# RWKV-7 layer of a four-layer trunk: k and r kept in memory, sixteen head pairs in one run with half 1's products, z and half 0's output projection between their matmuls

## The chip, the cores and the metric

One core of one Trainium2 chip runs the whole program. The metric is the device time of one execution in microseconds (us), here as the median of several runs; a profile is one further execution of the same program.

## The reference, cut to what matters

Four post-norm layers over `x` (1024 positions, 1024 channels, f32) run one after the other: short convolution, S5 state space, RWKV-7, short convolution. The change is in the third, and at the end of the second, where the third's first operands are built.

```
def _rwkv_step(state, inp):
    r_t, w_t, k_t, v_t, kk_t, a_t = inp
    sa = jnp.einsum("bhvk,bhk->bhv", state, -kk_t)
    state = (state * w_t[:, :, None, :] + sa[..., None] * (kk_t * a_t)[:, :, None, :]
             + v_t[..., None] * k_t[:, :, None, :])
    out = jnp.einsum("bhvk,bhk->bhv", state, r_t)
    return state, out
...
    dx = token_shift(x) - x
    xs = x[None] + dx[None] * mu[:, None, None, :]
    r, k, v, z = jnp.einsum("nbld,nde->nble", xs[:4], w_rkvz)
    xw, xa = xs[4], xs[5]
    w_log = -jax.nn.softplus(-(w0 + jnp.tanh(xw @ w1) @ w2)) - 0.5
    a = jax.nn.sigmoid(a0 + (xa @ a1) @ a2).astype(f32)
...
    return (out * jax.nn.silu(z)) @ w_out
```

There are 16 heads of 64 channels. After every mixer come r = alpha*x + mixer(x), a gate (`ple_gate`, `ple_proj`) and a LayerNorm.

## The kernel before, in words

The sequence is cut into two halves of 512 positions, and the channels into eight blocks m of 128, two heads each. A **product** is one 128x512 block of x @ W for one m and one half: 24 matmuls, because f32 operands are split into a high and a low part and three of the four cross products are taken (`mm3`, lines 308 to 310). Its weights come by one 512 KB load (`wload`, line 282), are split by ScalarE (line 285) and VectorE (line 286) and are fetched two blocks ahead, in the order of `weight_order`. The operands `xs[(s, h)]` (s = 0 r, 1 k, 2 v, 3 z) are made by `build`: `mix` on ScalarE and VectorE, then the split (`split_into`, line 191).

The recurrence is done in chunks of 64 positions, by **pair**: one m (two heads) in one half, 16 pairs in all. A pair has these parts, in `rwkv_layer` and `inner_setup`:

- `use_k`, `use_r`: from the k and r products in PSUM, with the decay and a read back from memory (`dCS`, `dA`), they make the scaled operands `ra`, `kb`, `ant`, `kbt` and the bonus `dBV`.
- `prep`: score matmuls (line 1700) and masks; `tsolve`: the inverses of 16x16 blocks on VectorE; `join`: those are put together to 64x64 inverses by small matmuls (zi 1780, ut 1789 and 1790, zp 1805, tp 1811).
- `seq`: eight chunks in a row. Each is a matmul with the state (line 1857), a copy by ScalarE (`uv`, 1858), a matmul (1861) and a state update by VectorE (1864), with `sd` from GpSimd (1856) beside it. Then come the output matmuls (1871), the group norm, the bonus and the product with silu(z) (1904), and a store to `dY`.

The order of the work is the order in which `rwkv_layer` writes it, rearranged by a scheduler that gives `prep`, `join`, `seq` and `tsolve` more or less priority (`prio`). Each engine then runs its own instructions strictly in that fixed order. All DMAs are issued by one queue, SyncE's, which also keeps its order and waits itself for the buffers and data that a DMA needs.

For each half in turn the layer does: `lora` (the two low-rank paths); eight z products with `use_z` (silu(z) to `dZ`, decay and a to `dCS`, `dA`); eight v products with `use_v`; then the eight pairs, each with its own k and r product written just ahead of the part that reads it. The recurrence of a pair runs while the next pair's k, r, `use_k` and `use_r` are done. After half 1's pairs the tail of the layer follows: output projection of half 0 (`w_out_unit`, tile `op`), gate of half 0 (`gate_half`, tiles `gp` and `pp`), output projection of half 1, gate of half 1.

Of the kernel before, what the change touches and what calls it, by code (L numbers as in the profile page):

```python
# [15 lines left out]
P = 128  # L16
NB = 8
# [211 lines left out]
def weight_order(layers):  # L229
# [16 lines left out]
    for l in layers:  # L246
# [10 lines left out]
        elif kind == 1:  # L257
            for ms in (range(NU), range(2 * NB)):
                blocks("ssm_w_in", (0,), ms)
            blocks("ssm_w_glu", (0,))  # L260
            blocks("ssm_w_out", (0,))
        else:
            for h in range(2):
                for i in (3, 2):
                    blocks("rwkv_w_rkvz", (0, i))
                for i, m in [(1, 0), (1, 1), (0, 0), (0, 1)] + [(i, m) for m in range(2, NB) for i in (1, 0)]:
                    add("rwkv_w_rkvz", (0, i), m * P)
            for h in range(2):
                blocks("rwkv_w_out", (0,))
                gate(l)  # L270
# [374 lines left out]
def ple_ln(S, l, last, nxt):  # L645
# [3 lines left out]
    for h in range(2):  # L649
        rp, s = gate_half(S, l, h, pT[h], f"{'a' if l % 3 == 1 else 'b'}{h}", bg,  # L650
                          GR if nxt == 2 else GP)
        bg = [ln_gen(S, l, h, rp, s, xn, last, nxt)]
        if h == 0 and nxt == 2:
            bg.append(build(S, xn, 3, 0))
# [368 lines left out]
IP, TP, TQ = 5,2,2  # L1023
AHEAD = 2
# [227 lines left out]
TAGS = ((("a0", "a1"), ("b1", "b1")), (("a0", "b1"), ("b1", "a0")))  # L1252
# [16 lines left out]
def mix(S, X, s, h, k):  # L1269
    C = S.rw  # L1270
    t = tt(S, "mix")
    x = X[k][h]
    S.nc.scalar.activation(t, x[:, 1:HT + 1], AF.Copy, scale=C.om[s][:, k:k + 1])
    S.nc.vector.scalar_tensor_tensor(t, x[:, 0:HT], C.mu[s][:, k:k + 1], t, ALU.mult, ALU.add)
    return t


def build(S, X, s, h):

    xs = S.rw.xs[(s, h)] = []  # L1280
    t0, t1 = TAGS[h][s in (0, 2)]
# [20 lines left out]
def rwkv_layer(S, X, bg, l, last, nxt):  # L1302
# [27 lines left out]
    def lora(h):  # L1330
        w12 = S.wp.tile([P, NB, P], F32, tag="wraw", name="w12", bufs=3)
        nc.sync.dma_start(w12[:, :, 0:64], A["rwkv_w1"][0].rearrange("(k p) n -> p k n", p=P))
        nc.sync.dma_start(w12[:, :, 64:P], A["rwkv_a1"][0].rearrange("(k p) n -> p k n", p=P))
# [3 lines left out]
        w2 = []  # L1337
        for nm in ("rwkv_w2", "rwkv_a2"):
# [20 lines left out]
        return L, w2  # L1359
# [5 lines left out]
    def use_z(m, h, ps, L, w2):  # L1365
        sg = T_("sg")
        SC.activation(sg, ps, AF.Sigmoid)
        V.tensor_tensor(sg, ps, sg, ALU.mult)
        nc.sync.dma_start(dZ[m][:, hs(h)], sg)
# [4 lines left out]
        for i, ps_ in enumerate((pw, pa)):  # L1374
            raw = w2[i][:, m * P:(m + 1) * P]
# [31 lines left out]
    def use_k(m, h, ps, R):  # L1407
        ga, cs = T_("ga"), T_("cs")
        nc.sync.dma_start(ga, dA[m][:, hs(h)])
        nc.sync.dma_start(cs, dCS[m][:, hs(h)])  # L1410
# [14 lines left out]
        V.tensor_tensor(kp, ps, kp, ALU.mult)  # L1425
        V.scalar_tensor_tensor(c3(aq), c3(ps), C.nkk[:, m:m + 1], pt[:, :, 0:CH], ALU.mult, ALU.mult)
# [25 lines left out]
        R.ant = slot(S, ("a0", "a1")[h], "ant")  # L1452
# [3 lines left out]
    def use_r(m, h, ps, R):  # L1456
        V.tensor_tensor(view(R.ra, 64, [[256, 4], [64, 2], [1, 64]]), c4(ps), c4pt(R.pt), ALU.mult)
        kp = R.kp
        V.scalar_tensor_tensor(kp, ps, vec("r_k")[:, m:m + 1], kp, ALU.mult, ALU.mult)

        R.kbt = []
        for g in range(2):
            pn = S.paux.tile([P, HT], F32, tag="aux", name="kbtp")
            for i in range(4):
                nc.tensor.transpose(pn[:, i * P:(i + 1) * P], R.kb[:, 4 * g + i, :], S.ident)
            t = slot(S, ("a0", "a1")[h], "kbt")
            SC.copy(t, pn)
            R.kbt.append(t.rearrange("p (a b) -> p a b", a=4))
        yield
# [9 lines left out]
        nc.sync.dma_start(dBV[m][:, hs(h)], kp)  # L1479
        yield  # L1480

    dBV = dram_list(S, "dBV", [P, T])
# [453 lines left out]
```

## Time and profile before

| | us |
|---|---|
| median of 3 runs | 2891.94 (2890.35 to 2897.93) |
| profiled execution, its own time | 2891.85 |
| its span, first to last instruction | 2890.1 |
| TensorE matmul busy in the span | 2732.9 (95%) |
| VectorE busy | 1825.3 (63%) |
| ScalarE busy | 1122.2 (39%) |
| GpSimd busy | 652.3 (23%) |

Busy times are sums over instructions of one engine; TensorE's matmuls overlap in its pipeline, and their ends are modelled. The granted clock is given as a share of full speed: 1.0 is 2.4 GHz, and the other level is half of it, 1.2 GHz, so that a mean of 0.85 over a stretch says that 30% of it ran at half speed. Stretches are given in us from the span's start: the RWKV layer's first product starts at 1154, half 0's pairs run to about 1656, half 1's z and v products follow, its pairs run from about 1765, the first output projection from about 2054, the first gate from 2142, the second output projection from 2198.

### The profile page before, as it was taken

What the parts mean: (1) busy time and instruction counts of PE and PEld (TensorE: products, weight loads), DVE (VectorE), ACT (ScalarE), POOL (GpSimd) and SP (SyncE); (2) the same over time, 40 slices, a digit from 0 to 9 for tenths busy, and PEclk for the clock granted to TensorE, in tenths of its full rate; (3) what the DMA queues carried; (4) which work ended last, traced back from release to release, by engine and by line L of the source; (5) the groups of instructions that cost most, each with busy time, mean ns of one, the idle gap of its engine ahead of it and who ended that gap; (6) DMA issues with size and microseconds to landing.
All of it is one profiled execution on the core that took longest, in us unless ns stands there. A gap on an engine that the chain in (4) does not pass through costs nothing. (4 is left out here: it accounts for less than half of the span.)

```text
span 2890.1 us, 47194 instructions
## 1 busy us (share of the span) xinstructions
PE 2732.9 (95%) x18331; PEld 2164.9 (75%) x18331; DVE 1825.3 (63%) x3396; ACT 1122.2 (39%) x2163; POOL 652.3 (23%) x772
## 2 busy tenths in 40 slices
PE   8999999999999999999887899988899999999998
PEld 6887788778877887676666576766677778888887
DVE  6787855476757348877666587766657473333654
ACT  3333322242254224665455575555434231112322
POOL 1243413121107033102333211333342210000000
PEclk9999999999999999999988799998899999999999
DMA  5333322257873234462222254222334332112321
GB/s 165 97 95 95 95 77 66 88 170 210 224 245 110 88 99 131 155 192 94 78 73 82 77 185 134 85 69 81 102 103 137 104 88 58 52 44 66 117 66 38
DMA packets 449776, 313.10 MB, mean 108 GB/s; under 512 B 48360, under 2 KB 393744, under 8 KB 449552
## 3 DMA queue, kind: packets, MB, share of 16 engines
q1 hardware_dynamic: 449552, 310.08, 35.8%
q8 instruction: 144, 2.36, 0.3%
q14 instruction: 80, 0.66, 0.1%
HBM read 240.28 MB, written 69.21 MB: 107 GB/s over the span
## 5 line engine op out<-in xcount | busy, mean ns | idle before, releaser
L285 ACT CAST wh<-wraw 128x1024 fp32r<-128x1024 f32 x283 | 297.2, 1050 | 699.3 <-PE gp L309 186.5
L286 DVE TENSOR_TENSOR wl<-wraw,wh 128x1024 fp32r<-128x1024 f32 x283 | 369.7, 1306 | 314.9 <-ACT wh L285 309.3
L1856 POOL TENSOR_SCALAR sd<-state,pc 128x128 f32<-128x128 f32 x128 | 94.9, 744 | 214.1 <-DVE state L1864 213.6
L1864 DVE SCALAR_TENSOR_TENSOR state<-p,pc,sd 64x64 f32<-64x64 f32 x256 | 72.2, 282 | 73.6 <-PE p L1861 62.0
L621 POOL TENSOR_TENSOR ln_s<-ln_s,rp 128x512 f32<-128x512 f32 x42 | 61.0, 1452 | 208.1 <-DVE rp L617 208.1
L1861 PE MATMUL p<-uv,kbt 128*128 128x128 f32 x256 | 67.2, 348 | 26.1 <-ACT uv L1858 24.4
L1861 PEld LDWEIGHTS p<-uv,kbt 128*128 128x128 f32 x256 | 44.3, 210 | 57.6 <-ACT uv L1858 49.6
L1857 PE MATMUL p<-state,ra 128*128 128x128 f32 x256 | 64.2, 336 | 15.7 <-DVE state L1864 15.0
L308 PE MATMUL zp<-x_0h,wh 128*128 128x512 f32 x192 | 76.8, 400 | 0.0
L310 PE MATMUL gp<-r_0h,wl 128*128 128x512 f32 x192 | 76.8, 400 | 0.0
L310 PE MATMUL gp<-r_1h,wl 128*128 128x512 f32 x192 | 76.2, 397 | 0.5 <-DVE wl L286 0.5
L1858 ACT COPY uv<-p 64x128 f32<-64x128 f32 x128 | 33.3, 261 | 111.5 <-PE p L1857 109.9
L308 PE MATMUL gp<-r_1h,wh 128*128 128x512 f32 x192 | 76.4, 398 | 0.0
L309 PE MATMUL gp<-r_0l,wh 128*128 128x512 f32 x192 | 76.3, 397 | 0.0
L1857 PEld LDWEIGHTS p<-state,ra 128*128 128x128 f32 x256 | 44.2, 208 | 42.6 <-DVE state L1864 31.2
L308 PE MATMUL gp<-r_0h,wh 128*128 128x512 f32 x192 | 76.1, 396 | 0.0
L308 PE MATMUL zp<-x_1h,wh 128*128 128x512 f32 x192 | 76.0, 396 | 0.0
L310 PE MATMUL zp<-x_0h,wl 128*128 128x512 f32 x192 | 75.8, 395 | 0.0
L310 PE MATMUL zp<-x_1h,wl 128*128 128x512 f32 x192 | 75.7, 395 | 0.0
L309 PE MATMUL zp<-x_1l,wh 128*128 128x512 f32 x192 | 75.7, 394 | 0.0
L309 PE MATMUL zp<-x_0l,wh 128*128 128x512 f32 x192 | 75.7, 394 | 0.0
L636 POOL TENSOR_TENSOR rp<-r_0h,r_0l 128x512 f32<-128x512 f32 x24 | 38.5, 1630 | 164.1 <-PE op L309 164.0
(755 smaller groups left out, 8429.4 us busy)
## 6 DMA issues: line engine op xcount, KB each, us to landing
wraw<-in_conv_w_in_dram SPq DMA_DIRECT2D x80, 512.0 KB
wraw<-in_rwkv_w_rkvz_dram SPq DMA_DIRECT2D x64, 512.0 KB
wraw<-in_ple_gate_dram SPq DMA_DIRECT2D x56, 512.0 KB
wraw<-in_conv_w_out_dram SPq DMA_DIRECT2D x24, 512.0 KB
wraw<-in_ssm_w_in_dram SPq DMA_DIRECT2D x21, 512.0 KB
xt<-xd SPq DMA_DIRECT2D x32, 256.0 KB
wraw<-in_rwkv_w_out_dram SPq DMA_DIRECT2D x16, 512.0 KB
wraw<-in_ple_proj_dram SPq DMA_DIRECT2D x14, 512.0 KB
```

The costliest lines, as they stand in the source:

```text
L285: nc.scalar.copy(wh, raw)
L286: nc.vector.tensor_tensor(wl, raw, f32(wh[:]), ALU.subtract)
L308: nc.tensor.matmul(ps, lh, xh, start=(k == 0), stop=False)
L309: nc.tensor.matmul(ps, lh, xl, start=False, stop=False)
L310: nc.tensor.matmul(ps, ll, xh, start=False, stop=(k == kt - 1))
L621: nc.gpsimd.tensor_tensor(s, s, rs, ALU.add)
L636: (eng or nc.gpsimd).tensor_tensor(rs, f32(rh[:]), f32(rl[:]), ALU.add)
L1856: G.tensor_scalar(sd, st, R.pc[:, c:c + 1], None, ALU.mult)
L1857: nc.tensor.matmul(p1, R.ra[:, c, :], st, start=False, stop=False, skip_group_check=True)
L1858: SC.copy(uv[rb, :], p1[rb, :])
L1861: last = nc.tensor.matmul(p2[:, 0:P], R.kbt[c // 4][:, c % 4, :], uv, start=True, stop=True)
L1864: V.scalar_tensor_tensor(st[cs, cs], p2[cs, cs], R.pc[cs, c:c + 1], sd[cs, cs], ALU.mult, ALU.add)
```

## The change

- The pairs of both halves run one after the other, 16 in a row. What half 1 needs ahead of them (`lora`, `use_w`, which is the decay and a part of `use_z`) is done before the first pair.
- k and r products no longer stand in the pair. Their blocks are copied from PSUM by ScalarE and stored (`use_d` to `dK`, `dR`); the pair loads them back (`kr`, `rr`) and works from SBUF.
- 60 products form a list, `FILL`: half 0's remaining k and r, half 1's v, k, r, then z of both halves, then half 0's output projection. `go(rate)` writes them between the parts of the pairs in thirds of a product, `RATE` products a pair (6, 5, then 3.5); `need` makes sure that a pair's k and r are done before it.
- z is stored without silu. `ys_build` makes silu(z) and the product with y, in half 0 by Exp, Ln and Exp, in half 1 by Sigmoid, with two multiplications on GpSimd.
- `build` makes the low part on GpSimd, not on VectorE. Half 1's x, and half 0's for the later builds, is not kept but loaded again block by block (`shifted`, tile `xr`, two buffers). In `use_r` the multiplication that makes half of `ra` moves from VectorE to GpSimd.
- The last pair's join and recurrence (`end`) run beside half 0's gate.
- PSUM: two buffers for products (three before), three for the small matmuls (two before). `sd` has one buffer (two before).

The parts that the text speaks of, cut:

```diff
@@ weight_order
-            for h in range(2):
-                for i in (3, 2):
-                    blocks("rwkv_w_rkvz", (0, i))
...
+            blocks("rwkv_w_rkvz", (0, 2))
+            for i, m, _ in LEAD + FILL:
+                add(*(("rwkv_w_out", (0,)) if i == OUT else ("rwkv_w_rkvz", (0, i))), m * P)
@@
+OUT = 4
+LEAD = [(1, 0, 0), (1, 1, 0), (1, 2, 0), (0, 0, 0)]
+FILL = [(1, 3, 0), (1, 4, 0), (1, 5, 0), (0, 1, 0), (1, 6, 0), (1, 7, 0)] + [(0, _m, 0) for _m in range(2, NB)] + \
+    [(_i, _m, _h) for _i, _h in ((2, 1), (1, 1), (0, 1), (3, 0), (3, 1), (OUT, 0)) for _m in range(NB)]
+RATE = (6, 5) + (3.5,) * 14
+SPOTS = 15
@@
+def shifted(S, h, k):
+    t = S.rg.tile([P, HT + 1], F32, tag="xr", name="xr", bufs=2)
+    if h == 0:
+        S.nc.gpsimd.memset(t[:, 0:1], 0.0)
+        S.nc.sync.dma_start(t[:, 1:], x_dram(S)[k][:, 0:HT])
+    else:
+        S.nc.sync.dma_start(t, x_dram(S)[k][:, HT - 1:T])
+    return t
@@ build
-        split_into(S, hl, t)
+        S.nc.scalar.copy(hl[0], t)
+        S.nc.gpsimd.tensor_tensor(hl[1], t, f32(hl[0]), ALU.subtract)
@@ rwkv_layer
-    S.pmm = ls.enter_context(S.tc.tile_pool(name="pmm", bufs=3, space=PSUM))
-    S.paux = ls.enter_context(S.tc.tile_pool(name="paux", bufs=2, space=PSUM))
+    S.pmm = ls.enter_context(S.tc.tile_pool(name="pmm", bufs=2, space=PSUM))
+    S.paux = ls.enter_context(S.tc.tile_pool(name="paux", bufs=3, space=PSUM))
...
-    def use_z(m, h, ps, L, w2):
-        sg = T_("sg")
-        SC.activation(sg, ps, AF.Sigmoid)
-        V.tensor_tensor(sg, ps, sg, ALU.mult)
-        nc.sync.dma_start(dZ[m][:, hs(h)], sg)
+    def use_w(m, h, L):
...
+    def use_d(dst):
+        def use(m, h, ps):
+            t = T_("st")
+            SC.copy(t, ps)
+            nc.sync.dma_start(dst[m][:, hs(h)], t)
+        return use
@@ use_k, use_r
+        kr = S.tmp.tile([P, HT], F32, tag="ln_s", name="kr", bufs=1)
+        nc.sync.dma_start(kr, dK[m][:, hs(h)])
...
-        V.tensor_tensor(view(R.ra, 64, [[256, 4], [64, 2], [1, 64]]), c4(ps), c4pt(R.pt), ALU.mult)
+        rr = T_("rr")
+        nc.sync.dma_start(rr, dR[m][:, hs(h)])
+        G.tensor_tensor(view(R.ra, 64, [[256, 4], [64, 2], [1, 64]]), c4(rr), c4pt(R.pt), ALU.mult)
@@
+    def go(thirds):
+        credit[0] += thirds
+        while credit[0] >= 1:
+            credit[0] -= 1
+            pull(F)
+
+    def need(*block):
+        while block not in done:
+            pull(F)
+            credit[0] -= 1
...
+        for q in range(NP):
+            m, h = q % NB, q // NB
...
+            rate = RATE[q] * 3 / SPOTS
+            need(1, m, h)
+            need(0, m, h)
+            for g in (use_k(m, h, R), use_r(m, h, R)):
+                for _ in g:
+                    pull(inner, IP)
+                    pull(tsol, TP)
+                    go(rate)
...
+            for _ in prio(I.prep(m, h, R), PJ):
+                go(rate)
+            if q > 0:
+                for _ in prio(I.join(*((q - 1) % NB, (q - 1) // NB), Rs[q - 1]), PJ):
+                    go(rate)
...
+    rp, s = gate_half(S, l, 0, pT[0], "a1", [end()], GT)
@@ seq
-            sd = rg.tile([P, P], F32, tag="sd", name="sd", bufs=2)
+            sd = rg.tile([P, P], F32, tag="sd", name="sd")
...
-        z = S.tmp.tile([P, HT], F32, tag="ln_v", name="zz", bufs=1)
-        nc.sync.dma_start(z, dZ[m][:, hs])
-        G.tensor_tensor(yt, yt, z, ALU.mult)
```

**TensorE, the seventh pair of half 1.** Before, these rows of its order hold chunks of one recurrence (1857, 1861), the seventh pair's prep (wps) and the join of the pair ahead of it (zi, ut, zp), with nothing else between them; the trace has them at about 2014.

```order
L1857 MATMUL p_19432<-state,ra 128x128
L1861 MATMUL p_19576<-uv,kbt 128x128
L1724 MATMUL wps<-uv,sca 64x64 x16
L1780 MATMUL zi<-t_19843,nz_9912 32x32 x32
L1782 MATMUL zi<-ident 32x256 x4
L1857 MATMUL p_19431<-state,ra 128x128
L1789 MATMUL ut<-zi,ub 32x32 x32
L1790 MATMUL ut<-ub,zi 32x32 x32
L1861 MATMUL p_19584<-uv,kbt 128x128
L1805 MATMUL zp<-t_19949,m_19213 32x32 x16
```

The same place in the changed kernel (lines 1815, 1871, 1873, 1880, 1881, 1896 and 1988 are the old 1724, 1780, 1782, 1789, 1790, 1805 and 1899, the transposes of a pair's output):

```order
L1815 MATMUL wps<-uv,sca 64x64 x16
L1871 MATMUL zi<-t_20280,nz_9928 32x32 x32
L1873 MATMUL zi<-ident 32x256 x4
L1566 MATMUL op<-ys_0h,wl 128x512
L1564 MATMUL op<-ys_0h,wh 128x512
L1565 MATMUL op<-ys_0l,wh 128x512
L1880 MATMUL ut<-zi,ub 32x32 x32
L1881 MATMUL ut<-ub,zi 32x32 x32
L1988 MATMUL otp<-ident,o 128x128 x4
L1896 MATMUL zp<-t_20400,m_19514 32x32 x16
L1566 MATMUL op<-ys_0h,wl 128x512
L1564 MATMUL op<-ys_0h,wh 128x512
```

Three matmuls of half 0's output projection now stand between zi and ut, and more behind zp; the recurrence's chunks have moved out of the join.

**SyncE's queue, one pair.** Before, around half 0's fourth pair: its `ga` and `cs` loads, then a state store, loads for `uv`, weights, and the bonus and z loads of an earlier pair.

```order
L1409 DMA ga<-dA_9744 128x512
L1410 DMA cs<-dCS_9736 128x512
L1876 DMA dST_9781<-state 128x128
L1691 DMA uv<-dVT_9776 64x512 x2
L282 DMA wraw<-in_rwkv_w_rkvz_dram 128x8x128
L1894 DMA bv<-dBV_9799 128x512
L1905 DMA dY_9765<-yt 128x512
L1896 DMA zz<-dZ_9758 128x512
```

In the changed kernel, around half 0's seventh pair (lines 1436, 1437 and 280 are the old 1410, 1409 and 282):

```order
L1436 DMA cs<-dCS_9739 128x512
L1425 DMA dK_9784<-st 128x512
L1437 DMA ga<-dA_9747 128x512
L1290 DMA xr<-xd_5283 128x513
L280 DMA wraw<-in_rwkv_w_rkvz_dram 128x8x128
L1484 DMA rr<-dR_9795 128x512
L1425 DMA dK_9785<-st 128x512
L1434 DMA kr<-dK_9788 128x512
L1290 DMA xr<-xd_5284 128x513
```

Two loads of x (`xr`) and two stores of half 1's k now stand among the pair's loads, and `kr` and `rr` have been added to them.

## Rows read from the trace of the kernel before

**Rows 1.** The page: busy time by engine, and two of its 40-slice lines.

```profile
PE 2732.9 (95%) x18331; PEld 2164.9 (75%) x18331; DVE 1825.3 (63%) x3396; ACT 1122.2 (39%) x2163; POOL 652.3 (23%) x772
...
PE   8999999999999999999887899988899999999998
...
PEclk9999999999999999999988799998899999999999
```

**Rows 2.** Busy time by stretch of the RWKV layer: stretch, length, each engine's busy time.

```profile
core 0: us, PE busy (x) PEld busy (x) DVE busy (x) ACT busy (x) POOL busy (x), PEclk, DMA share, GB/s
1154.00:1285.00 131.00, 128.51 (x551) 93.75 (x551) 106.53 (x166) 81.04 (x136) 9.20 (x9) 0.99 0.56 181
1285.00:1379.00 94.00, 83.77 (x1041) 61.53 (x1039) 73.55 (x163) 58.18 (x132) 24.17 (x33) 1.00 0.31 96
1379.00:1603.00 224.00, 184.93 (x2720) 143.52 (x2722) 151.44 (x384) 117.09 (x324) 76.72 (x103) 0.85 0.24 75
1603.00:1656.00 53.00, 43.57 (x548) 28.06 (x545) 30.54 (x74) 27.07 (x66) 13.18 (x17) 0.79 0.31 88
1656.00:1765.00 109.00, 104.67 (x494) 82.20 (x493) 77.13 (x123) 66.77 (x128) 9.78 (x9) 0.98 0.55 176
1765.00:1857.00 92.00, 80.31 (x1100) 59.61 (x1100) 74.80 (x170) 54.98 (x120) 25.34 (x32) 0.98 0.30 88
1857.00:1997.00 140.00, 127.27 (x1707) 99.35 (x1708) 91.17 (x243) 70.24 (x204) 45.51 (x60) 0.88 0.25 77
1997.00:2048.00 51.00, 38.52 (x517) 31.01 (x516) 28.78 (x77) 23.72 (x66) 17.26 (x22) 0.70 0.19 57
2048.00:2142.00 94.00, 86.30 (x1125) 64.20 (x1126) 57.49 (x141) 44.62 (x135) 34.19 (x41) 1.00 0.37 118
2142.00:2198.00 56.00, 56.00 (x243) 45.12 (x242) 31.76 (x33) 20.05 (x28) 21.11 (x15) 1.00 0.45 141
```

**Rows 3.** The same view, TensorE's matmuls of products (tile sp) alone.

```profile
1285.00:1379.00 94.00, 50.67 (x175) 1.00 0.31 96
1379.00:1603.00 224.00, 72.39 (x206) 0.85 0.24 75
1857.00:1997.00 140.00, 61.36 (x177) 0.88 0.25 77
```

**Rows 4.** The same view, matmuls of half 0's output projection (tile op) alone.

```profile
2048.00:2142.00 94.00, 56.17 (x192) 1.00 0.37 118
```

**Rows 5.** The same view, all engines, in the last layer, where products run back to back.

```profile
2425.00:2525.00 100.00, 100.00 (x432) 80.91 (x431) 30.65 (x39) 17.24 (x23) 8.34 (x10) 1.00 0.17 48
```

**Rows 6.** Groups of instructions by line: the scan that makes the decay's sums.

```profile
L1385 DVE TENSOR_TENSOR_SCAN cs<-reset,sw 128x512 f32<-128x512 f32 x16 | 20.8, 1298 | 5.3 <-ACT sw L1381 5.3
```

**Rows 7.** Who waited for whom, TensorE, 1285 to 2048: total us, times, longest.

```profile
PE p L1861 <- ACT uv L1858: 23.7, 24, 5.4
PE otp L1899 <- POOL o L1892: 13.6, 11, 2.4
PE p L1857 <- DVE state L1864: 13.3, 16, 2.2
PE ut L1789 <- ACT zi L1786: 10.4, 9, 3.3
```

**Rows 8.** Groups by line again: instructions of the kinds that the change adds.

```profile
L1445 POOL TENSOR_TENSOR kb<-kp,cs 128x512 f32<-128x512 f32 x16 | 21.9, 1369 | 1.5 <-DVE kp L1425 1.5
...
L191 DVE TENSOR_TENSOR xs1l<-mix,xs1h 128x512 fp32r<-128x512 f32 x16 | 10.5, 690 | 1.2 <-ACT xs1h L191 1.1
...
L1390 ACT COPY v<-sp 128x512 f32<-128x512 f32 x16 | 9.3, 581 | 1.9 <-PE sp L310 1.9
```

**Rows 9.** Line 286, the weights' low part, 1703 to 1765, then 1857 to 1997: min/median/max ns.

```profile
L286 DVE TENSOR_TENSOR wl<-wraw,wh x10: 1215/1226/1227, 1704.0 to 1757.9; 128x1024 fp32r<-128x1024 f32 x10
...
L286 DVE TENSOR_TENSOR wl<-wraw,wh x7: 1183/1237/2341, 1870.2 to 1979.6; 128x1024 fp32r<-128x1024 f32 x7
```

**Rows 10.** SyncE: one DMA's issue, then the queue's waits, 1285 to 2048.

```profile
L1369 SPq DMA_DIRECT2D dZ<-sg x16: 319/320/679, 1177.2 to 1705.9; - x16
...
SPq L282 <- DVE wl L286: 125.0, 31, 14.2
...
SPq L1477 <- PE pss L1422: 59.3, 10, 14.2
```

More of the change, by code (lines that the diff above doesn't have):

```diff
@@ L653, in ple_ln @@
         if h == 0 and nxt == 2:
-            bg.append(build(S, xn, 3, 0))
+            bg.append(build(S, xn, 2, 0))
     return xn, bg
@@ L1479, in use_r @@
         nc.sync.dma_start(dBV[m][:, hs(h)], kp)
+        R.kbt = []
+        for g in range(2):
+            pn = S.paux.tile([P, HT], F32, tag="aux", name="kbtp")
+            for i in range(4):
+                nc.tensor.transpose(pn[:, i * P:(i + 1) * P], R.kb[:, 4 * g + i, :], S.ident)
+            t = slot(S, R.tags[0], "kbt")
+            SC.copy(t, pn)
+            R.kbt.append(t.rearrange("p (a b) -> p a b", a=4))
         yield
-    dBV = dram_list(S, "dBV", [P, T])
     def c4pt(pt):
@@ new lines, in rwkv_layer, with fill @@
+    stages = [(2, 1), (1, 1), (0, 1), (3, 0), (3, 1), (OUT, 0)]
+    mk = lambda i, h: ys_build(h) if i == OUT else build(S, X, i, h)
+    def fill():
+        for i, m, h in FILL:
+            if (i, h) in stages and m == 0:
+                while builds:
+                    pull(builds)
+                n = stages.index((i, h)) + 1
+                if n < len(stages):
+                    builds.append(mk(*stages[n]))
+            if (i, m, h) == (0, 2, 0):
+                builds.append(mk(*stages[0]))
+            for _ in product(i, m, h):
+                yield
+            pull(builds, 2 if m == 0 or (i, m, h) == (0, 2, 0) else 1)
@@ new lines, in rwkv_layer @@
+    F = [fill()]
+    credit = [0.0]
+    def go(thirds):
[7 more added lines that the diff above has]
+            credit[0] -= 1
+    if (2, 0) not in xs:
+        for _ in build(S, X, 2, 0):
+            pass
+    Ls = []
+    lora_setup()
+    for _ in lora(0, Ls):
+        pass
+    I = inner_setup(S, rg, T_)
+    builds.append(build(S, X, 1, 0))
+    for m in range(NB):
+        for _ in product(2, m, 0):
+            pass
+        use_w(m, 0, Ls[0])
+        pull(bg, ZP[m])
+        pull(builds, BV[m])
@@ new lines, in rwkv_layer @@
+    while bg:
+        pull(bg)
+    while builds:
+        pull(builds)
+    for k in range(NB):
+        X[k][1] = None
+    builds.append(build(S, X, 0, 0))
+    lo = [lora(1, Ls)]
+    for i, m, h in LEAD[:3]:
+        for _ in product(i, m, h):
+            pull(lo)
+            pull(builds)
+    while lo:
+        pull(lo)
+    while builds:
+        pull(builds)
+    lead = product(*LEAD[3])
+    for m in range(NB):
+        use_w(m, 1, Ls[1])
+        if m in (1, 3, 5):
+            next(lead)
@@ L1627, in rwkv_layer, with end @@
+    def end():
+        yield from rest(NP - 1)
+        rgs.close()
+        region_b(S, True)
+        pT.append(prep_p(S, l, 1, None))
+        yield
+        yield from ys_build(1)
+    pT = [prep_p(S, l, 0, [slot_split(S, "a1", f"pT{i}") for i in range(2)])]
+    rp, s = gate_half(S, l, 0, pT[0], "a1", [end()], GT)
     lng = [ln_gen(S, l, 0, rp, s, xn, last, nxt)]
     for m in range(NB):
-        w_out_unit(S, wprep(S, "rwkv_w_out", (0,), m * P), ys, resid, tags[1][1], m, 1)
+        w_out_unit(S, wprep(S, "rwkv_w_out", (0,), m * P), ys, resid, "b1", m, 1)
@@ L1887, in seq @@
         yield
-        if m == NB - 1:
+        if h and m >= NB - 2:
             rsqrt(S, rg.tile([P, 8], F32, tag="rs_t8", name="rs_t", bufs=2), s1, s2)
```

289 lines of the change are left out of this document (121 added, 168 removed).

## The prediction

> **What bounds the kernel now.** I read the page first. Its busy line has TensorE at 2732.9 us of a span of 2890.1, 95%, with VectorE at 63% [rows 1]; so TensorE is the engine to look at, and no other comes near. The two slice lines say that this is not the same everywhere: full busy digits and a clock digit of 9 at both ends, digits of 7 and 8 in the middle, in the RWKV layer [rows 1]. The next view is therefore the busy time by stretch of that layer [rows 2]. A stretch loses time in two ways: TensorE is idle, or its clock is at the half level. With length L, busy time B and clock c, I count (L - B) + (1 - c) x B as lost. From 1154 to 2198, a length of 1044, this gives, stretch by stretch: 4, 10, 67, 19, 6, 13, 28, 24, 8 and 0 us, **179 us lost** in all, and 865 us of work at full clock [rows 2]. The worst is 1379 to 1603, half 0's pairs: 39 idle, and 0.15 x 185 = 28 for the clock.
>
> What goes with the loss is how much of a stretch is products. One product costs 24 x 100/432 = 5.55 us where products run back to back [rows 5]. From 1379 to 1603 there are 206 product matmuls, 8.6 products, 48 us, 21% of the stretch; 30% is lost. From 1857 to 1997 they are 29%, and 20% is lost. From 1285 to 1379 they are 43%, and 11% is lost, all of it idle at clock 1.00 [rows 2, 3]. From 2048 to 2142 the eight products of the first output projection run beside the last pairs: 47%, and 8% lost, again at clock 1.00 [rows 2, 4]. The ends of both halves, 1603 to 1656 and 1997 to 2048, where the products have run out, lose 35% and 47% [rows 2]. So TensorE is bound by its own work where products stand between the steps of a pair, and by the steps where they don't. The waits say which steps: the second matmul of a chunk on ScalarE's copy, the output transposes on GpSimd, the join on ScalarE [rows 7].
>
> **The change, part by part.** *TensorE's work.* The program's order has 14,180 matmuls in both kernels, and from 1154 to the second output projection both do the same ones. Cost 0: the 865 us stay, and only the 179 can go. That is the ceiling of the gain.
>
> *The start.* By 1285 the old kernel has done 18 products (16 of z and v, two of k), 100 us of 127 us of work; 27 us are `lora`, decay matmuls and transposes of one half. The new one does 12 products and those parts for both halves: 12 x 5.55 + 54 = 120 us. Half 1's decay work has one product as cover for eight blocks. The bound from above is that TensorE stands still for one scan a block, 8 x 1.3 = 10 us [rows 6], from below 0; with few products near, I take 10, and 4 as before: 14 lost. The pairs then begin at 1154 + 134 = 1288, about where they did.
>
> *The pairs.* What is left is 865 - 120 = 745 us, of which the first gate has 56 [rows 2]: 689 us of work in sixteen pairs, 60 products (333 us) and 356 us of the pairs' own, 22 a pair. (The last recurrences, some 17 us, slip beside the gate; I leave them here.) If x is the lost share, the run lasts 689/(1 - x), and the products are 333 us of it. At x = 0.11 it lasts 774 us with 43% products, which is just the share that lost 11% [rows 2, 3]: consistent. Lost: 85 us. The drain between the halves has gone, since the sixteen follow each other, and the drain at the end lies beside the gate. The bounds are 8%, 60 us, and 14.5% as from 1765 to 1857, 117 us [rows 2, 4].
>
> *The gate* now has a recurrence or two between its matmuls. It lost 0; 56 of 73 us would be products, 77%, far above 47%. I take 0, with the order's last recurrence matmul well ahead of the gate's end.
>
> *ScalarE, VectorE, GpSimd.* In the run GpSimd gets 40 splits (five of the operand sets), 16 halves of `ra`, 16 multiplications for half 0's silu, and loses 16: 56 x 1.4 = 78 us more on top of some 210 [rows 2, 8]. VectorE loses 56 x 0.69 = 39 us. ScalarE gets 44 copies of k, r and z, 44 x 0.58 = 26 us, and 24 passes for silu, 14 us [rows 8]. None comes near 774 us: from 1285 to 2048 VectorE has about 527, ScalarE 418. Off the path: 0, unless it delays a step (below). That k and r are read from SBUF and not PSUM has no row; the kinds of instruction are the same, 0 either way.
>
> *SyncE's queue.* Some 100 DMAs more at 0.32 us of issue are 32 us [rows 10], beside a run of 774: 0. The stores and loads of k and r lie many products apart.
>
> *Buffers.* Two PSUM buffers for products: a product's copy has until the next but one begins, some 12 us at 3.5 products in 48 us. 0 expected; at worst a wait of one copy, 60 x 0.58 = 35 us [rows 8]. `sd` with one buffer: the next one needs the state that its last reader writes. 0.
>
> **The sum.** Lost after: 14 + 85 + 0 = 99 us, against 179: 80 us gained. The profiled execution took 2891.85, the median is 2891.94, so the offset is nothing: **2812 us**. With 8% and 14.5% it is 2787 and 2844.
>
> **Rivals.**
>
> *Fuller than any stretch shown.* The products are written in thirds between all parts of a pair, more evenly than at 1285. If only 5% is lost, that is 36 us: 14 + 36 = 50, 2763 us. For it: half 1's products stretch, 1656 to 1765, loses 6% at most [rows 2]. Against: a matmul that waits holds up the products behind it, too.
>
> *The helpers are late.* The longest waits of TensorE are for ScalarE, GpSimd and VectorE in the recurrence and behind it, 61 us in four rows [rows 7], and ScalarE and GpSimd get more to do. If these waits come half as long again on top of the forecast, with some of the clock's loss, 45 us: 2857 us.
>
> *A port.* The weights' low part took 1226 ns where GpSimd was idle; where GpSimd worked it had the same median, 1237, and a longest of 2341 [rows 9]. So a GpSimd instruction in the way can double such a VectorE instruction, but seldom did. Should half of the added 78 us of GpSimd land in a pair's steps, it is 39 us: 2851 us. The Trainium skill, SBUF — State Buffer, "Who interferes with whom", would have it more often: a VectorE instruction with two SBUF inputs and a GpSimd one that reads SBUF shut each other out entirely, and reading k and r from SBUF makes more of these. By that rule the whole 78 us would count, and the time would be 2890 us; the medians speak against it.
>
> *Slower: the queue.* One queue issues all DMAs in order. Among a pair's loads now stand loads of x that wait for one of two buffers, which a build deep in ScalarE's, VectorE's and GpSimd's queues gives back. If `kr` or `cs` comes late, `use_k`'s first matmuls hold up TensorE. The queue has waited up to 14.2 us for a VectorE split, and as long for a buffer of a pair [rows 10]. From 80/16 = 5 us a pair it turns the gain into a loss; at 10 us a pair the time is 2812 + 160 = 2972 us. Against: those long waits were there before, and no matmul's wait for a load is among the longest [rows 7].
>
> *Nothing.* The cover is there, but the losses of pairs come back to what they were, in waits and clock: 2892 us.
>
> **How the numbers follow.** Forecast (2787 to 2844) 0.52; fuller 0.12; late helpers 0.14; port 0.10; nothing 0.04; queue 0.08. The range 2755 to 2865 takes in the forecast, and nearly all of the fuller, helper and port cases; the rest leaves about 0.18 out. About 0.3%, 9 us, can be told from no change: faster 0.88, same 0.04, slower 0.08.
>
> **What would show it.** In the changed profile: the clock at 1.0 through the pairs, TensorE idle for about a tenth of that run, a spacing of pairs of about 48 us with 3.5 products in each, the first gate at about 2062 and the second output projection at about 2118, and no stretch like 1997 to 2048. The queue's case would show the matmuls `pss`, which need `kr`, late in every pair; the helpers' case the rows of ScalarE's `uv` copy and of the output transposes grown; the port's case a median of the weights' low part well above 1.24 us. The forecast is wrong if the pairs lose over 15% at 43% products, or if the first pair starts well after 1288.

## The result, and the profile after

The changed kernel takes 2914.08 us (median of 5 runs, 2905.87 to 2916.57), the kernel before 2891.94 (5 runs, 2890.35 to 2897.93); the ratio is 1.0064, 95% interval 1.0042 to 1.0085. It is **slower by 0.6%**, where 2812 us was forecast. The profiled execution took 2916.57 us, its span is 2914.5.

The page, its busy line and the same two slice lines as [rows 1]:

```profile
PE 2734.4 (94%) x18331; PEld 2144.5 (74%) x18331; DVE 1811.7 (62%) x3300; ACT 1141.3 (39%) x2208; POOL 800.1 (27%) x874
...
PE   8999999999999998989988989988996999999998
...
PEclk9999999999999999999999999999998999999999
```

The long dip of the clock has gone from the middle, as meant. GpSimd has gained 148 us where VectorE lost 14. Busy time by stretch, as in [rows 2], for the start, half 1's decay work, the run of pairs, the first gate, a stop, and the second output projection:

```profile
1154.00:1276.00 122.00, 109.76 (x435) 70.54 (x436) 102.28 (x145) 76.13 (x131) 36.59 (x41) 0.95 0.54 178
1276.00:1312.00 36.00, 27.02 (x89) 18.49 (x87) 15.82 (x28) 20.66 (x44) 2.08 (x3) 0.81 0.52 177
1312.00:2111.00 799.00, 711.01 (x8809) 535.14 (x8808) 552.41 (x1223) 447.26 (x1111) 323.50 (x352) 0.94 0.40 128
2111.00:2200.00 89.00, 80.19 (x708) 60.97 (x707) 38.98 (x81) 33.98 (x84) 37.42 (x41) 0.96 0.28 87
2200.00:2212.00 12.00, 0.44 (x1) 0.44 (x2) 3.53 (x5) 3.93 (x7) 8.07 (x6) 0.53 0.68 219
2212.00:2270.00 58.00, 50.89 (x212) 39.70 (x211) 47.98 (x71) 23.96 (x37) 25.89 (x19) 0.95 0.34 109
```

By the prediction's formula the lost time is 18 + 14 us at the start, 131 in the run (16.4% of 799), 12 + 12 at the gate: 187 us up to the second output projection, against 179 before. That projection then lasts 58 us, where it took 49 before (2198 to 2247). So the pairs did lose less than before, and the start and the end took it back: the loss was moved, and not reduced.

Who waited for whom, TensorE, 1312 to 2111, against [rows 7] (line, what it waited for, total us, times, longest):

```profile
PE p L1948 <- DVE state L1955: 23.8, 29, 2.4
PE pb L1493 <- POOL kpl L1491: 17.1, 14, 2.5
PE otp L1988 <- POOL o L1983: 8.2, 7, 2.5
PE ut L1880 <- ACT zi L1877: 6.3, 9, 1.7
...
PE p L1952 <- ACT uv L1949: 4.6, 3, 1.8
```

The wait for ScalarE's `uv` fell from 23.7 us to 4.6: the products cover it, that is, they stand in TensorE's order while the copy is made. The wait for the state has grown from 13.3 us. The second row is as good as new. It is for the low part of kp, which GpSimd makes ahead of `pb`, two matmuls with a matrix of ones that sum kp for the bonus. In the kernel before, 1285 to 2048, the same wait was

```profile
PE pb L1475 <- POOL kpl L1473: 0.8, 2, 0.4
```

The groups of GpSimd's instructions in the changed kernel, 1312 to 2111:

```profile
L1947 POOL TENSOR_SCALAR sd<-state,pc 128x128 f32<-128x128 f32 x116 | 98.8, 851 | 175.6 <-DVE state L1955 169.5 <-issue 3.5 <-DMA dK<-st 2.6
L1485 POOL TENSOR_TENSOR ra<-rr,pt 128x512 f32<-128x512 f32 x16 | 26.6, 1664 | 1.6 <-DMA rr<-dR 1.6
...
L1491 POOL TENSOR_TENSOR kpl<-kp,kph 128x512 fp32r<-128x512 f32 x16 | 23.4, 1462 | 4.4 <-ACT kph L1490 4.4
L1302 POOL TENSOR_TENSOR xs3l<-mix,xs3h 128x512 fp32r<-128x512 f32 x16 | 23.0, 1440 | 26.3 <-ACT xs3h L1301 21.1 <-DVE state L1955 5.2
```

And the layer's end, TensorE's longest wait in 2160 to 2260, and what ScalarE did then (timeline: start, us, line, tiles, idle before):

```profile
PE op L306 <- ACT sg L613: 15.6, 1, 15.6
```

```profile
2206.01 0.62 ACT L191 CAST ys_1h<-yl 128x512 fp32r<-128x512 f32 x1 [2.71 <-POOL yl L1546]
2206.54 0.62 ACT L1544 ACTIVATE sz<-zl 128x512 f32<-128x512 f32 x1
2209.88 0.62 ACT L191 CAST ys_1h<-yl 128x512 fp32r<-128x512 f32 x1 [2.71 <-POOL yl L1546]
2210.40 0.62 ACT L1544 ACTIVATE sz<-zl 128x512 f32<-128x512 f32 x1
2210.93 0.58 ACT L613 ACTIVATE sg<-gp 128x512 f32<-128x512 f32 x1
...
2226.22 0.62 ACT L191 CAST ys_1h<-yl 128x512 fp32r<-128x512 f32 x1 [1.33 <-POOL yl L1546]
```

The gate's last sigmoid stands behind half 1's ys, whose casts wait for two GpSimd multiplications each. TensorE waits for it before it can begin the second output projection: `op` doesn't read the sigmoid, but by the code it takes the PSUM buffer that the sigmoid reads, the pool for products having two. That wait isn't the whole of it. The projection's first product needs all eight blocks of ys, and the eighth is cast at 2226.22 only. The rows show why they come so slowly: the sigmoid of a block (`sz`) stands behind the cast of the block ahead, so that the steps of a block run one after the other, 3.9 us from one `sz` to the next.

### The profile page after: what moved, and what is told of

It reads as the page before. It is cut to its first block, busy times and chain, and to the rows that moved or that the text cites. A ratio compares the mean times of both kernels' runs of the same rounds, so it can differ in the third digit from the quotient of the medians.

```text
span 2914.5 us, 47517 instructions
## 1 busy us (share of the span) xinstructions
PE 2734.4 (94%) x18331; PEld 2144.5 (74%) x18331; DVE 1811.7 (62%) x3300; ACT 1141.3 (39%) x2208; POOL 800.1 (27%) x874
## 5 line engine op out<-in xcount | busy, mean ns | idle before, releaser
L284 DVE TENSOR_TENSOR wl<-wraw,wh 128x1024 fp32r<-128x1024 f32 x283 | 371.4, 1312 | 301.6 <-ACT wh L283 294.6
L1947 POOL TENSOR_SCALAR sd<-state,pc 128x128 f32<-128x128 f32 x128 | 106.5, 832 | 187.3 <-DVE state L1955 181.0
L1948 PE MATMUL p<-state,ra 128*128 128x128 f32 x256 | 59.7, 316 | 26.1 <-DVE state L1955 23.8
L307 PE MATMUL gp<-r_1l,wh 128*128 128x512 f32 x192 | 75.1, 391 | 0.0
L439 POOL TENSOR_TENSOR cv<-cv,sg 128x512 f32<-128x512 f32 x24 | 34.9, 1455 | 136.4 <-DVE sg L438 136.3
```

Source lines behind the costliest of these rows:

```text
L284: nc.vector.tensor_tensor(wl, raw, f32(wh[:]), ALU.subtract)
L307: nc.tensor.matmul(ps, lh, xl, start=False, stop=False)
L439: nc.gpsimd.tensor_tensor(cvs[h], cvs[h], sg, ALU.mult)
L1947: G.tensor_scalar(sd, st, R.pc[:, c:c + 1], None, ALU.mult)
L1948: nc.tensor.matmul(p1, R.ra[:, c, :], st, start=False, stop=False, skip_group_check=True)
```

## The experiments

The theory to begin with: the change's order does what was forecast, and what it did beside that (steps moved to GpSimd, `pb` ahead of the transposes of kb, few products as cover at both ends) takes the gain back. The rivals: the loss lies at the ends alone; VectorE is the late helper; the waits come whatever the placement. Ratios are to the kernel before, on the same chip; the changed kernel has 1.0064, and 0.001 is 2.9 us.

**ys on VectorE** (e1_ys_dve both halves, e5_ys0_dve half 0 alone).

```diff
-            G.tensor_tensor(z, z, s, ALU.mult)
-            G.tensor_tensor(y, y, z, ALU.mult)
+            V.tensor_tensor(z, z, s, ALU.mult)
+            V.tensor_tensor(y, y, z, ALU.mult)
```

> Edit: the two multiplications that build each block of ys (z*s, y*z) run on VectorE instead of GpSimd, in both halves. Theory 'the end': in the changed kernel TensorE waits 15.6 us once, at 2196, for a sigmoid that stands in ScalarE's queue behind the last half's ys, whose two GpSimd multiplications take about 4.1 us a block in series, and 17.1 us of half clock follow at 2201; with VectorE's about 0.7 us each the wait goes and the last output projection starts some 20 to 25 us earlier, so 2889 to 2897 us. Theory 'the pairs' (the lost time is the helpers' lateness inside the sixteen pairs): the end gives 8 us at most, since the clock and the gates take it back, and the first half's ys, which lies beside the pairs, puts 11 us more on VectorE there: 2906 to 2918 us. If both hold, the span from the first pair to the first gate (799 us) stays and only the end shrinks.

> Edit: as e1_ys_dve, but only the first half's ys (built beside the last head pairs) goes to VectorE; the second half's stays on GpSimd. e1_ys_dve gained 0.9% of the kernel before against the changed kernel (ratio 0.9974 against 1.0064), and its trace puts 24 us of that before the first gate and 6 to 8 behind it. Theory 'pairs' (GpSimd's queue delays the steps of the last pairs): this run keeps most of it, ratio 0.998 to 1.001. Theory 'end' (the serial GpSimd multiplications of the second half hold ScalarE and the PSUM tile): this run keeps little, ratio 1.004 to 1.007.

Measured: 0.9974 (0.9961 to 0.9988) and 0.9993 (0.9979 to 1.0007). Half 0's ys alone, beside the last pairs, gives 0.7 of the 0.9%. At the end the wait only shrank, in e1_ys_dve:

```profile
PE op L306 <- ACT sg L613: 10.3, 1, 10.3
```

The run of pairs takes 775 us in e1_ys_dve (1309 to 2084), where it took 799. So the larger cost was in the pairs, and my first reading of the end was a minor part. These edits do more than undo: the product of y and z stood on GpSimd in the kernel before, too (`yt<-yt,zz`), and what moving it would give there was not tried.

**The other GpSimd steps on VectorE** (e2_split_ra_dve both edits; e11_ra_dve the second alone, e12_split_dve the first alone).

```diff
-        S.nc.scalar.copy(hl[0], t)
-        S.nc.gpsimd.tensor_tensor(hl[1], t, f32(hl[0]), ALU.subtract)
+        split_into(S, hl, t)
...
-        G.tensor_tensor(view(R.ra, 64, [[256, 4], [64, 2], [1, 64]]), c4(rr), c4pt(R.pt), ALU.mult)
+        V.tensor_tensor(view(R.ra, 64, [[256, 4], [64, 2], [1, 64]]), c4(rr), c4pt(R.pt), ALU.mult)
```

> Edit: the low part of build's split and use_r's half of ra go back from GpSimd to VectorE (about 1.5 us of GpSimd per block for ra, 1.7 for the split; 0.7 us of VectorE in their place). Theory 'GpSimd is the late helper of the pairs': TensorE's 17.1 us for the low part of kp, 8.2 for o and part of the 23.8 for the state (its decay is a GpSimd product) shrink, 10 to 30 us less: 2884 to 2904 us. Theory 'VectorE is the late helper' (552 of 799 us busy in the pairs, it makes the state, the masks and the solve's products): 0 to 15 us slower, 2914 to 2929 us. Theory 'the order of the instructions on TensorE, not the load of a helper, makes the waits': no change within 6 us.

> Edit in the changed kernel: only the half of ra goes back to VectorE (16 instructions of 1.66 us on GpSimd, 27 us in the pairs). Theory 'GpSimd steps that a pair's own matmuls wait for': this one carries most of the 0.7% that e2_split_ra_dve gained, ratio 0.999 to 1.002. Rival 'the load on GpSimd as a whole': it carries the smaller part, in proportion to its share of the time taken off (27 of 27 + 57 us), ratio 1.003 to 1.005.

> Edit in the changed kernel: only build's low parts go back to VectorE (40 instructions of about 1.4 us on GpSimd in the pairs, 57 us). Theory 'GpSimd steps that a pair's own matmuls wait for': little, ratio 1.004 to 1.007. Rival 'the load on GpSimd as a whole': the larger part of 0.7%, ratio 0.999 to 1.003.

Measured: 0.9997 (0.9981 to 1.0013) for both, 1.0015 (1.0002 to 1.0029) for `ra`, 1.0007 (0.9995 to 1.0019) for the low parts. Each alone gives 0.5 to 0.6%, both 0.7%. Neither of the two theories fits both: `ra`, a third of the time taken off, gives nearly as much as the low parts, and these, which no pair reads, are not free. With intervals of 0.1 to 0.2% on each ratio, the order of the three gains is not settled. What is plain is that the relief of GpSimd pays and VectorE's load doesn't show.

**The transposes of kb first again** (e3_kbt_first): a block of lines moved, as it stood before.

```diff
         V.scalar_tensor_tensor(kp, rr, vec("r_k")[:, m:m + 1], kp, ALU.mult, ALU.mult)
+        R.kbt = []
+        for g in range(2):
...
+        yield
         pb = S.paux.tile([P, HT], F32, tag="aux", name="pb")
...
-        R.kbt = []
-        for g in range(2):
```

> Edit: in use_r the eight transposes of kb stand ahead of the two ones-products for kp again, as in the kernel before, so that the split of kp has 1.2 us of TensorE work and a yield to finish in. Theory 'order': TensorE's new wait for the low part of kp (14 times, 17.1 us) and the one for its high part (5.6 us) go, and with them some of the half-clock dips in the pairs: 12 to 25 us less, 2889 to 2902 us. Theory 'load' (the helpers are late whatever stands ahead): the wait moves to the state or to o, 2908 to 2918 us.

Measured: 1.0032 (1.0016 to 1.0048), a gain of 9 us, less than expected. The wait for kpl went from the list, and the one for `o` took its place, 21.7 us where it was 8.2 (same view and stretch as above):

```profile
PE otp L1988 <- POOL o L1983: 21.7, 13, 2.9
PE p L1948 <- DVE state L1955: 19.7, 34, 1.6
```

**More cover at the start** (e4_lead8).

```diff
+LEAD = [(1, 0, 0), (1, 1, 0), (1, 2, 0), (0, 0, 0), (1, 3, 0), (1, 4, 0), (1, 5, 0), (0, 1, 0)]
+FILL = [(1, 6, 0), (1, 7, 0)] + [(0, _m, 0) for _m in range(2, NB)] + \
...
+RATE = (4, 3) + (3.5,) * 14
...
+    lead = [product(*b) for b in LEAD[3:]]
     for m in range(NB):
         use_w(m, 1, Ls[1])
-        if m in (1, 3, 5):
-            next(lead)
+        pull(lead, 2)
```

> Edit: eight products instead of four run ahead of the pairs; the five that are left after the builds are spread as cover between the eight use_w steps of half 1, and the first two pairs pull two products fewer each. Theory 'start': the changed kernel loses 9 us at 1276 to 1312 (27 of 36 us busy, clock 0.81) and 8 us at 1154 to 1276; covered, 8 to 15 us less: 2899 to 2906 us. Theory 'cover only moves' (the products taken from the first two pairs leave those pairs as poor as the start was, and the pairs lose what the start gains): 2910 to 2920 us.

Measured: 1.0061 (1.0044 to 1.0079), no gain: with these pairs, cover only moves.

**Together** (e6_pool_free is e1 and e2; e7_pool_free_kbt adds e3; e8_o_dve puts the scaling of `o` on VectorE too; e10_all_lead8 adds e4).

```diff
-        G.tensor_tensor(o, o, bcs(s1), ALU.mult)
+        V.tensor_tensor(o, o, bcs(s1), ALU.mult)
```

> Edit: e1_ys_dve and e2_split_ra_dve together: all the multiplications and low parts that the changed kernel gave to GpSimd in these stages are back on VectorE. Theory 'GpSimd is the late helper': the two gains (0.9% and 0.7%) add up but for what they share in the last pairs, ratio 0.988 to 0.994 (2855 to 2872 us where the kernel before takes 2888). Rival 'VectorE is full next': VectorE is then busy some 73% of the pairs, and the second move gives back what it gains: ratio 0.996 to 1.000.

> Edit: e6_pool_free with the transposes of kb ahead of the ones-products for kp, as in e3_kbt_first, which alone gained 0.3% of the kernel before: its 17.1 us wait for the low part of kp went, but the wait for o (a GpSimd product) grew from 9.6 to 23.5 us. Theory 'order and load are separate': with GpSimd free the wait for o does not grow, and this run is 0.3 to 0.6% below e6_pool_free. Rival 'one wait replaces another': the same as e6_pool_free within 0.2%.

> Edit: e7_pool_free_kbt with the product that scales o (1.4 us on GpSimd, once a pair, waited for by the transposes of o) on VectorE too. Theory 'GpSimd steps on TensorE's path': the wait for o (6 to 23 us in the earlier runs) falls under 4 us and the kernel gains another 0.2 to 0.5%. Rival 'VectorE is full': no gain, or up to 0.3% slower, with the wait for the state growing instead.

> Edit: e8_o_dve with e4_lead8's eight products ahead of the pairs. Theory 'start': 0.2 to 0.5% below e8_o_dve, ratio 0.977 to 0.980, since the start still loses some 20 us (137 of 160 us busy at clock 0.91). Rival 'cover only moves', which e4_lead8 bore out in the changed kernel (1.0061 against 1.0064): ratio 0.980 to 0.984.

Measured: 0.9927 (0.9910 to 0.9943), 0.9844 (0.9827 to 0.9861), 0.9816 (0.9794 to 0.9839), 0.9771 (0.9749 to 0.9794). e10_all_lead8, 2823.08 us where the kernel before took 2888.92 beside it, beats both kernels. The order of the transposes, worth 0.3% alone, is worth 0.8% with GpSimd free, since the wait for `o` grows less in its place (9.8 to 15.7 us over 1300 to 2190, where it went from 9.6 to 23.5); the cover at the start, worth nothing alone, 0.45%. These last steps are small: the intervals of e7_pool_free_kbt and e8_o_dve overlap, and those of e8_o_dve and e10_all_lead8 touch. In e8_o_dve, 1302 to 2008, TensorE's first waits are

```profile
PE p L1947 <- DVE state L1954: 14.4, 24, 1.4
PE ut L1879 <- ACT zi L1876: 7.3, 8, 1.8
PE otp L1987 <- DVE o L1982: 6.9, 9, 1.2
```

Busy time of start, pairs and end, in this order: before, the changed kernel, e7_pool_free_kbt, e8_o_dve, e10_all_lead8 (for e6_pool_free, placed behind the changed kernel, the pairs alone).

```profile
1145.00:1290.00 145.00, 135.24 (x575) 98.02 (x574) 120.53 (x183) 91.33 (x152) 17.18 (x26) 0.98 0.57 179
1290.00:2142.00 852.00, 745.25 (x9223) 567.22 (x9223) 579.91 (x1362) 457.66 (x1162) 246.14 (x314) 0.91 0.31 96
2142.00:2302.00 160.00, 158.12 (x694) 127.51 (x693) 102.53 (x133) 56.51 (x79) 48.73 (x34) 1.00 0.39 120
```

```profile
1145.00:1312.00 167.00, 138.94 (x530) 90.10 (x528) 125.45 (x178) 101.64 (x181) 47.68 (x49) 0.91 0.54 175
...
2111.00:2326.00 215.00, 186.79 (x1152) 143.96 (x1152) 114.91 (x184) 75.78 (x145) 83.32 (x72) 0.94 0.33 102
```

```profile
1306.00:2067.00 761.00, 689.15 (x8810) 515.34 (x8811) 554.45 (x1296) 447.78 (x1112) 241.67 (x282) 0.97 0.42 134
```

```profile
1143.00:1306.00 163.00, 140.93 (x530) 92.25 (x528) 127.42 (x199) 100.93 (x182) 17.53 (x27) 0.90 0.56 181
1306.00:2015.00 709.00, 651.83 (x8324) 488.98 (x8325) 538.15 (x1226) 429.87 (x1056) 220.96 (x267) 0.97 0.45 141
2015.00:2251.00 236.00, 212.51 (x1637) 161.05 (x1636) 148.91 (x269) 91.38 (x199) 76.58 (x71) 0.95 0.33 102
```

```profile
1302.00:2008.00 706.00, 653.45 (x8324) 491.59 (x8325) 548.13 (x1239) 430.20 (x1057) 202.60 (x254) 0.98 0.45 142
2008.00:2243.00 235.00, 215.28 (x1637) 162.81 (x1637) 151.65 (x272) 91.34 (x199) 69.08 (x68) 0.94 0.33 102
```

```profile
1143.00:1311.00 168.00, 150.25 (x593) 101.99 (x591) 130.28 (x201) 106.03 (x186) 15.50 (x26) 0.94 0.60 191
1311.00:1993.00 682.00, 628.55 (x8274) 475.54 (x8274) 538.55 (x1238) 428.42 (x1053) 206.18 (x255) 0.99 0.45 143
1993.00:2231.00 238.00, 213.15 (x1624) 162.23 (x1624) 148.79 (x270) 89.76 (x197) 71.11 (x66) 0.94 0.32 99
```

Lost time from these rows by the same formula (the clock's rounding leaves some 3 us open in the pairs):

| | start | pairs | share of the pairs' stretch | end |
|---|---|---|---|---|
| before | 12 | 174 | 20.4% | 2 |
| changed | 41 | 131 | 16.4% | 39 |
| e6_pool_free | | 93 | 12.2% | |
| e7_pool_free_kbt | 36 | 77 | 10.8% | 34 |
| e8_o_dve | | 66 | 9.3% | 33 |
| e10_all_lead8 | 27 | 60 | 8.8% | 38 |

The run of pairs is taken to the first gate's first matmul, and in the last three kernels more of the last pairs' work falls behind that point (1624 to 1637 matmuls in the end, 1152 in the changed kernel). So the sums of the three stretches compare more safely than the pairs alone: 188, 211, 147 and 125 us for before, changed, e7_pool_free_kbt and e10_all_lead8.

From the changed kernel to e6_pool_free the pairs lose 38 us less, of which idle time is 16 (88 to 72) and the clock 22 (43 to 21), though the wait for kpl is the same there (16.5 us). The wait for the state fell from 23.8 to 15.7 us; the rest is spread over small rows and fewer falls of the clock to half.

**The side edits in the old order** (c1_before_o_dve: e8's last edit; c2_before_pool: build's low part on GpSimd, and `pb` ahead of the transposes; c3_before_order: only the latter).

```diff
-        split_into(S, hl, t)
+        S.nc.scalar.copy(hl[0], t)
+        S.nc.gpsimd.tensor_tensor(hl[1], t, f32(hl[0]), ALU.subtract)
```

> Edit in the kernel before the change: the product that scales o moves from GpSimd to VectorE, as in e8_o_dve; nothing else. TensorE waits 13.6 us for o there between 1285 and 2048. Theory 'the restructured order is what gains': the old order gains little from a single freed step, ratio 0.996 to 1.000, so that e8_o_dve's 0.9816 is the change's own for the most part. Rival 'the gain is the placement, whatever the order': ratio 0.990 to 0.995.

> Edit in the kernel before the change: the low part of build's split goes to GpSimd and the ones-products for kp stand ahead of the transposes of kb, the two side edits that the change also makes; the loops stay as they are. In the changed kernel, undoing its GpSimd steps and this order was worth 2.0% (ratio 1.0064 to 0.9844). Theory 'side edits cost wherever they are': slower by 0.3 to 1.0%, ratio 1.003 to 1.010. Rival 'they cost only where products fill all of TensorE's gaps': same within 0.2%.

> Edit in the kernel before the change: only the order, the ones-products for kp ahead of the transposes of kb; build's low part stays on VectorE. c2_before_pool, which has both, was 0.9% slower, and in its trace TensorE waits 8.7 us for low parts from GpSimd and 5.2 us for the step behind the ones-products, which the kernel before does not show. Theory 'the load on GpSimd costs the old order too, the position of the transposes little': ratio 0.999 to 1.003. Rival 'the position costs it': ratio 1.004 to 1.009.

Measured: 0.9948 (0.9930 to 0.9965), 1.0091 (1.0070 to 1.0112), 1.0018 (0.9998 to 1.0038). By the difference of the last two, the low parts on GpSimd cost the old order about 0.7%, 21 us. Two of TensorE's waits in c2_before_pool, 1306 to 2060, have grown from 2.2 and 1.9 us in the kernel before (1285 to 2048), where VectorE made the low part:

```profile
PE sp L308 <- DVE aq L1427: 9.7, 5, 2.6
...
PE sp L309 <- POOL xs0l L1286: 4.8, 7, 1.8
```

Only the second is a wait for a low part; the first, for VectorE's step that reads a k product, is 5.7 us in c3_before_order too (1290 to 2060), without the low parts. The larger part lies ahead of the pairs, where operands are built, too: the first `pss` starts at 1305.6, against 1290.3 before and 1289.2 in c3_before_order, and c2_before_pool's start loses 27 us, where the kernel before lost 12:

```profile
1145.00:1306.00 161.00, 141.13 (x583) 100.51 (x581) 119.95 (x157) 96.09 (x157) 57.84 (x55) 0.95 0.51 160
```

So this control shows a cost of such a placement, but not that of the pairs. And the scaling of `o` gains the old order 0.5%, so e8_o_dve's last step isn't the change's own. Taken against c1_before_o_dve, e8_o_dve is 0.9816/0.9948 = 0.987, about 38 us for the new order. That is the most it can be: the old order was given one of these placements back, not all (ys is one that was not tried there).

**The end** (e13_all_tail: e10_all_lead8 with the last gate's operands prepared behind half 1's ys).

```diff
-        pT.append(prep_p(S, l, 1, None))
-        yield
         yield from ys_build(1)
+        pT.append(prep_p(S, l, 1, None))
+        yield
```

> Edit: e10_all_lead8 with the second gate's own operands (four loads, eight transposes, two splits) prepared behind the second half's ys instead of ahead of it. In e10_all_lead8 the last pair's output is there at 2090 us and the first ys step runs at 2104. Theory 'ys is late because of what stands ahead of it': 6 to 14 us less, ratio 0.972 to 0.975. Rival 'the store and load of y alone take that long': same as e10_all_lead8 within 0.2%, ratio 0.975 to 0.979.

Measured: 0.9794 (0.9778 to 0.9811), not better than e10_all_lead8. So that isn't why ys is late. In e10_all_lead8 the wait for the sigmoid is only 1.2 us, and the end still loses 38 us; what would shorten it stays open.

## Why the prediction was wrong, step by step

**TensorE's work, cost 0: right.** B x c over the first five stretches above, up to the second output projection, is 872 us, against 865 forecast, and the page counts 18331 matmuls for both kernels. Everything that went wrong is lost time.

**The start, 14 us lost, pairs at 1288: wrong.** 32 us were lost, and the pairs began at 1312. 18 of them went ahead of half 1's decay work, where 4 were forecast. I bounded that work by one VectorE scan a block, 10 us; with one product as cover, 1276 to 1312 lost 14 us, and the clock fell to 0.81 in it, which the bound left out. The wait was another one, too, for ScalarE's copies of the small weights (`w`):

```profile
PE pw L1396 <- ACT w L1394: 6.0, 5, 1.3
```

e10_all_lead8 shows that cover there can be bought, once the pairs can do without it.

**The pairs, 11% lost: wrong for the changed kernel, near for its order.** It was 16.4%, above the 15% that was named as the sign of failure. With the GpSimd steps and the transposes undone it is 10.8% (e7_pool_free_kbt). That this is 11% almost to the digit is partly luck, since more of the last pairs lies beside the gate there than in the forecast. The rule from old stretches, lost share by products' share, came near only once the helpers were used as they had been in them; I had carried it over to another placement.

**ScalarE, VectorE, GpSimd, "off the path: 0, unless it delays a step": the step that failed.** I added up busy times and saw that none came near the run's length. The GpSimd steps cost 1.4%, 40 us (1.0064 to 0.9927), half 0's and half 1's ys included. The sum was short as well, 324 us of GpSimd in the run where it had 288, but even 324 are 40% of 799. Busy share says nothing of when a step is done.

**Overlooked: the order in `use_r`.** The diff also moved the transposes of kb behind `pb`. They had covered kpl; my sum has no term for it. It is worth 0.3% alone, and 0.8%, 24 us, with GpSimd free (0.9927 to 0.9844). In the old order it costs 0.2% by its ratio, and the interval (0.9998 to 1.0038) takes in nothing.

**The gate, 0: wrong.** 24 us were lost up to 2212 and about 9 in the projection behind it; before, the same end lost 2. I looked at the last recurrence, and not at what comes between it and the second projection: half 1's ys. Even in the best version the end loses 38 us.

**What is left.** From 2812 to 2914 are 102 us. Undoing the GpSimd steps and the order of the transposes gives back 64 (1.0064 to 0.9844). Of the rest, the start and the end, which lose 36 and 34 us in e7_pool_free_kbt where 14 and 0 were forecast, are more than enough.

**Rivals.** "The helpers are late", put at 2857 us, names what happened, but not how. Its signs, the rows of `uv` and of the output transposes grown, did not show: both fell (23.7 to 4.6 and 13.6 to 8.2 us), and the waits for kpl and the state grew in their place. It was also undersized, since I priced it by lengthening old waits. "The port" was put at 2851, and at 2890 by a rule: the Trainium skill, SBUF — State Buffer, "Who interferes with whom". The sign I named for it, the median of the weights' low part, did not move against [rows 9] (1312 to 2111: min/median/max ns):

```profile
L284 DVE TENSOR_TENSOR wl<-wraw,wh x59: 1181/1225/2287, 1313.7 to 2104.1; 128x1024 fp32r<-128x1024 f32 x59
```

But a median was a poor sign: 12 of these 59 instructions took over 1.4 us, 7 of 47 before (1285 to 2048), 3 of 59 in e6_pool_free (1306 to 2067), and GpSimd's side shows it, too (last section). That 2890 is nearer to 2914 than 2851 says little, since the start, the transposes and the end have their part in the miss. How much of the 40 us is such exclusion and how much plain queueing, these runs do not tell apart. "The queue" is not seen: no wait of TensorE for a load is among its rows, and the first `pss` of a pair comes about every 50 us (48 forecast): the 16 pairs' first and last of these matmuls start at

```profile
L1448 PE MATMUL pss<-c_ones_r,sq x128: 165/251/353, 1311.7 to 2063.1; 128*128 128x2 f32 x128
```

that is 751 us for fifteen spacings. "Buffers, 0" holds in the pairs, where the one row for a copy of a product (`sp <- st`) is 1.0 us; at the gate's end the 15.6 us for the sigmoid are a wait for a product's PSUM buffer, by the code. A third buffer was not tried. "Nothing", 2892 us, has about the right loss and the wrong places: the pairs gained, the start and the end lost.

## What to carry to other kernels

Read a diff for every edit that rides along with its main idea, and price each engine's new steps by who waits for them and what covers them, not by busy share. When a restructured kernel disappoints, undo the side edits in groups as well as singly: here 0.9, 0.7, 0.3 and 0%, 1.9% in all, became 2.9% together, of which the scaling of `o`, not tried by itself in the changed kernel, has some 0.3. The two GpSimd groups gave no more together (1.4%) than singly; the order of the transposes did (0.8 for 0.3%), since a wait that goes lets the next one show. And run the same side edit in the old kernel, so that its gain isn't credited to the new order.

## What the runs showed of the hardware

Where a GpSimd instruction and a VectorE one of two SBUF inputs overlapped, one of them took much longer, and in these rows it is the one that found the other at work. In e8_o_dve, timeline of VectorE and GpSimd around 1484 and 1540:

```profile
1483.83 2.32 DVE L284 TENSOR_TENSOR wl<-wraw,wh 128x1024 fp32r<-128x1024 f32 x1
...
1483.71 1.35 POOL L1470 TENSOR_TENSOR kb<-kp,cs 128x512 f32<-128x512 f32 x1
...
1539.51 1.23 DVE L284 TENSOR_TENSOR wl<-wraw,wh 128x1024 fp32r<-128x1024 f32 x1
1540.66 0.69 DVE L191 TENSOR_TENSOR xs0l<-mix,xs0h 128x512 fp32r<-128x512 f32 x1
1541.77 0.28 DVE L1954 SCALAR_TENSOR_TENSOR state<-p,pc,sd 64x64 f32<-64x64 f32 x1 [0.42 <-POOL sd L1946]
...
1539.65 2.08 POOL L1946 TENSOR_SCALAR sd<-state,pc 128x128 f32<-128x128 f32 x1 [1.63 <-DVE state L1954]
```

`sd`, 594 ns at its shortest, began 0.14 us behind the split `wl` and took 2.08 us, past the end of the next split as well, and the state update waited for it; VectorE's two kept 1.23 and 0.69 us. The other way round, `wl`, 1224 ns by its median there, began 0.12 us behind `kb` and took 2.32 us, while `kb` took 1.35 (median 1286 ns). This agrees with the rule of the Trainium skill named above, that the two engines lock each other out of a shared port pair. The median of `sd` over the pairs, 606 ns before, was 1026 ns in e8_o_dve, whose time is the better by 1.8% all the same:

```profile
L1946 POOL TENSOR_SCALAR sd<-state,pc x108: 594/1026/2143, 1302.3 to 2006.9; 128x128 f32<-128x128 f32 x108
```

So a longer `sd` is not what decides. The other thing: behind the 15.6 us wait at 2196, TensorE's next stretch ran at the half level, 1.2 GHz, while it was fully busy, so that the stop cost, by an estimate from this row, some 3 us (0.48 x 6) more than its own length:

```profile
2212.00:2218.00 6.00, 6.00 (x15) 4.41 (x14) 2.03 (x3) 1.15 (x2) 5.82 (x5) 0.52 0.53 177
```
